# A delta-rule scan whose rounds are written in two halves, with each state product beside one piece of a score product

## The chip, the cores and the metric

The kernel runs on one core of a Trainium2 chip. Its time is the device time of one execution in microseconds; three runs of the kernel before are given, and the profile is of one execution of its own. PE is the matrix engine (PEld its weight loads), DVE the vector engine, ACT the scalar engine, POOL the general-purpose engine, SP the engine that issues most DMAs.

## The reference

One layer of a bidirectional mixer works on 128 context tokens and 2048 latent tokens of 1024 channels. A normalised and modulated input goes through one projection; half of the channels take a gated short convolution, the other half a recurrent scan with 8 heads of 64 channels, in both directions:

```python
def step(S, inp):
    r_t, w_t, k_t, v_t, kk_t, a_t = inp
    s_kk = jnp.einsum('bdhij,bdhj->bdhi', S, kk_t)
    S = (S * w_t[..., None, :] - s_kk[..., :, None] * (kk_t * a_t)[..., None, :]
         + v_t[..., :, None] * k_t[..., None, :])
    return S, jnp.einsum('bdhij,bdhj->bdhi', S, r_t)

s_final, ys = lax.scan(step, s0.astype(f32), xs)
y = ys[:, 0] + jnp.flip(ys[:, 1], axis=1)      # after ys = jnp.moveaxis(ys, 0, 2)
```

The sum of both directions is normalised per head, gated, joined with the convolution half, multiplied with an output matrix, added to the input and normalised. Outputs are both token streams and the final context states.

## The kernel before, in words

Phase 1 computes norm, projection, convolution and the operands of the scan. Phase 3, at the end, is the output product. Phase 2 between them is the scan in chunks of 64 tokens, and the change lies there.

**Stages.** A stage takes a pair of heads (of four pairs) and eight chunks in each direction. Four blocks of eight chunks for each of four pairs, and one stage for the context, make 17 stages, numbered 0 to 16. In every stage there are two groups, `gi` 0 and 1, one for each direction, and each group's eight chunks are in two halves, n = 0 and 1, of four chunks.

**The products of a stage.** F and G (`partW`, tiles psF and psG) are products of the loaded operands, one pair of PSUM tiles (one for each group) for each half n. U and W (`partU`, psU and psW) complete the inverse of a 64 by 64 triangle from 32 by 32 blocks which POOL has solved (`solve`, result zt in DRAM, read back as zc, transposed on DVE as zr); ACT writes the inverse into the one buffer zb. X (`partB`, psX) multiplies F with zb, and ACT copies its negative into the buffer fg. E (`partB`, psE) multiplies parts of fg into the chunk matrices E: for each half n four pieces, two chunks of one group in each. A DVE multiplication with a mask (L1109) and an ACT copy take a piece out of PSUM, one behind the other. S (`partS`, psS) is the recurrence: for chunk i it multiplies E of that chunk with the state and the values in the tile sv, and DVE scales the result by the decay into the next chunk's sv (L1147), for which the next S waits. After chunks 3 and 7 the output half of psS goes into a tile y: copied by ACT in the first of the two visits to a block, added by DVE (L1164) in the second. T (`finish`, psT) transposes a finished y after its normalisation (DVE L1198 to L1217). S uses E of half 0 in chunks 0 to 3 and of half 1 in chunks 4 to 7.

**A round.** Round s runs the eight S of stage s and, between them, the end of `partB` of its own stage and F, G, U, W and the start of `partB` of stage s + 1. The parts are generators, and a string of letters says which generator takes its next step: L is `partW`, u and U `partU`, b `partB` of the own stage, B that of the next stage, S one chunk of `partS`, f the first three steps of a waiting `finish` and T its rest. There are three such strings: `ROUND`, `ROUND_END` for round 15, and eight S for round 16. While the flag `O.line` holds, PE takes its products in exactly this order (`mm`, `tr` and `behind`). DVE, ACT, POOL and SP are placed by a scheduler that plans the program when it is built, and each works through its own list in order.

**Buffers.** The products F, G, U, W, X, E and T take PSUM tiles from two pools in turn (`ps_tile`: two of one pool, three of the other), so that a tile can be written when the fifth one before it has been read out. From stage 14 on the pool of two is closed, and there are three. The S products have three tiles of their own. zb, zc and zr are single. The solving of stage s + 7 is written at the end of round s; POOL takes these one after the other. Its input ab is fetched by SP (L925) when the buffer of the solution two stages before is free, and what SP issues later waits behind that.

Of the kernel before, what the change touches and what calls it, by code (L numbers as in the profile page):

```python
# [745 lines left out]
NST = 17  # L746
LA = 3


ROUND = "f b L L S u b S b S S U S T U S L S B S L B B".split()  # L750
ROUND_END = "f b L L u S b S b S U S T U S L L S B S B B S".split()

def phase2(K):
    nc, tc, A, S = K.nc, K.tc, K.A, K.S
    V, G, P, T = nc.vector, nc.gpsimd, nc.scalar, nc.tensor
# [323 lines left out]
    def partB(s, st):  # L1081
        for n in range(2):
            px = [ps_tile([128, 4, 128], f"psX{s}_{gi}_{n}") for gi in range(2)]
            for i in range(4):
                for gi, g in enumerate(st.g):
                    u = half(g, n).start + i
                    for h in range(2):
                        r = place(g.d, h)
                        mm(px[gi][H[1 - h], i, :], B.zb[r, gi, u, :], g.F[n][r, i, :])
            for gi, g in enumerate(st.g):  # L1090
                for h in range(2):
                    copy(g.fs[H[1 - h], g.io, h, half(g, n)], px[gi][H[1 - h]].rearrange("p u (b t) -> p b u t", b=2), True)
            yield
            for h2 in range(2):
                for gi, g in enumerate(st.g):
                    if h2 == 0:
                        g.E.append(tl([128, 4, 2, 128], "E", 4))
                    us = half(g, n)
                    k = (h2 if g.d == 0 else 1 - h2) * 2
                    lt, rt = (g.fs, g.gs) if g.d == 0 else (g.gs, g.fs)  # L1100
                    pe = ps_tile([128, 2, 2, 128], f"psE{s}_{gi}_{n}{h2}")
                    for i in range(2):
                        u = us.start + k + i
                        for hd in range(2):
# [4 lines left out]
                    V.tensor_tensor(to(H[1]), of(H[1]), B.mE[:, g.d].unsqueeze(1).broadcast_to((128, 4, 64)), ALU.mult)  # L1109
                    copy(to(H[0]), of(H[0]))  # L1110
                yield

    def partS(s, st, nxt):

# [139 lines left out]
    def main():  # L1254
        setup_rest()
        run = lambda gen: [None for _ in gen]
        states(0, sts[0])
        sts[1] = partL(1)
        bb = B.bb
        O.line = True  # L1260
        next(bb)
        sts[2] = partL(2, K.first)
        partI(6, K.first)
        next(bb)
        sts[LA] = partL(LA, K.first)
        partI(7, O.solved)
        tail = iter(())
        for s in range(NST):
            st = sts.pop(s)
            more = s + 1 < NST  # L1270
            nil = iter(())
            W, uu = (partW(s + 1, sts[s + 1]), partU(s + 1, sts[s + 1])) if more else (nil, nil)
            own, bb = bb, partB(s + 1, sts[s + 1]) if more else nil
            todo = [pend.pop(0) for _ in range(len(pend) if s > NST - 4 else min(1, len(pend)))]
            if s == NST - 3:
                O.pm.close()
                O.pm = None
# [10 lines left out]
            gens = dict(L=W, b=own, u=uu, U=uu, B=bb, S=partS(s, st, sts.get(s + 1)))  # L1288
            for c in (ROUND if s < NST - 2 else ROUND_END if more else "S" * 8):
                if c == "f":  # L1290
                    for f in todo:
                        for _ in range(3):
                            next(f, None)
                elif c == "T":
                    for f in todo:
                        run(f)
                else:
                    next(gens[c])
                    if c == "S":
                        next(tail, None)  # L1300
# [211 lines left out]
```

## Time and profile before

| what | us |
|---|---|
| three timed runs | 1645.6, 1651.7, 1653.2 (median 1651.73) |
| span of the profiled execution, first to last instruction | 1642.5 |
| profiled execution's own time as the page gives it | the span alone, 1642.5 |
| PE busy in the span | 1531.9 (93%) |
| DVE, ACT, POOL busy | 1104.6 (67%), 762.7 (46%), 586.8 (36%) |
| first S product starts at | 1010.3 |
| last S product starts at | 1449.0 |

The scan runs from about 1010 to 1450 us; what stands ahead of it is phase 1, what follows is mostly the output product. In the rows below, a row of the timeline has the start in us, the duration, engine, line, operation, what it writes and reads, shape, how many in one run, and in brackets the engine's idle time before it with what ended that. A matrix product of F32 stands as two records, and an instruction's end on PE is modelled, so the time from the start of one group to the start of the next is what a group costs.

### The profile page before, as it was taken

To read this page: it belongs to the slowest core of one execution; us is meant where nothing else is said; L and a number is where in the kernel's file an instruction comes from. 1 tells how busy PE (TensorE), PEld (TensorE's weight loads), DVE (VectorE), ACT (ScalarE), POOL (GpSimd) and SP (SyncE) were. 2 spreads that over 40 slices of the span, in tenths; PEclk is the share of its full clock that TensorE was granted. 3 is DMA by queue.
4 is the path that set the end of the run, shared out by engine and by line. 5 is a ranking of instruction groups with operands and counts; after the bars stand their busy time and mean duration, and the time that the engine had idled before them with its cause. 6 is when DMAs were issued, how large, how long until landed. Compare 5 with 4: busy or idle time off the path is not lost.

```text
span 1642.5 us, 42385 instructions
## 1 busy us (share of the span) xinstructions
PE 1531.9 (93%) x17160; PEld 1405.2 (86%) x17160; DVE 1104.6 (67%) x2220; ACT 762.7 (46%) x1617; POOL 586.8 (36%) x1040
## 2 busy tenths in 40 slices
PE   5899999999999999999989999989999988789998
PEld 2899988999999999999988898878888876668886
DVE  5876978784738685658788794566776764574333
ACT  4554565554425452425554023757666673432222
POOL 0011211110112021102667474888888832022221
PEclk8899999999999999999999999999999998889999
DMA  9677668664746564656867858767767663264342
GB/s 377 202 272 251 237 222 300 212 230 179 236 156 195 176 210 149 203 182 203 275 203 228 285 173 256 183 166 188 215 169 202 185 160 93 66 199 166 122 151 93
DMA packets 237988, 327.23 MB, mean 199 GB/s; under 512 B 91288, under 2 KB 191896, under 8 KB 223712
## 3 DMA queue, kind: packets, MB, share of 16 engines
q1 hardware_dynamic: 231840, 318.55, 61.3%
q0 software_dynamic: 1200, 3.93, 0.6%
q8 instruction: 135, 2.21, 0.6%
q10 hardware_dynamic: 4752, 2.04, 0.5%
q14 instruction: 61, 0.50, 0.1%
HBM read 207.92 MB, written 116.54 MB: 198 GB/s over the span
## 4 chain that ended last, share of the span: by engine, by line
PE 45%; POOL 9%; DVE 8%; ACT 4%; issue 4%; DMA 3%; SPq 0%; DVEq 0%; POOLq 0%; ACTq 0%
POOL zt L950 4%; PE psu L1381 4%; PE psu L1382 4%; PE psu L1383 4%; POOL ztmp L947 3%; PE psE L840 2%; PE psS L840 2%; ACT fg L829 1%; PE mmc L166 1%; PE mmg L168 1%; PE mmg L166 1%; PE mmg L167 1%; PE mmc L167 1%; PE mmc L168 1%; PE mmv L166 1%
## 5 line engine op out<-in xcount | busy, mean ns | idle before, releaser
L950 POOL TENSOR_TENSOR zt<-zt,ztmp 128x30 f32<-128x30 f32 (+7 forms) x390 | 153.0, 392 | 30.6
L840 PE MATMUL psE<-fg 128*64 128x128 f32 x2176 | 135.4, 277 | 15.8 <-ACT fg L831 13.6
L840 PEld LDWEIGHTS psE<-fg 128*64 128x64 f32 x2176 | 120.6, 139 | 22.4 <-ACT fg L831 15.6
L840 PE MATMUL psS<-sv,E 128*64 128x64 f32 x2176 | 98.6, 233 | 19.0 <-DVE sv L1147 18.5
L840 PEld LDWEIGHTS psS<-sv,E 128*64 128x64 f32 x2176 | 81.6, 143 | 34.8 <-DVE sv L1147 24.9
L329 POOL TENSOR_TENSOR shk<-rawl 128x384 f32<-128x384 f32 (+1 forms) x24 | 23.5, 979 | 241.1 <-ACT rawl L325 221.8
L829 ACT ACTIVATE fg<-psX 64x512 f32<-64x512 f32 x136 | 80.5, 592 | 37.3 <-PE psX L840 35.2
L1448 POOL TENSOR_TENSOR z<-z,x 128x512 f32<-128x512 f32 x32 | 41.8, 1307 | 137.9 <-DVE z L1444 114.4
L947 POOL TENSOR_TENSOR ztmp<-ab,zt 128x60 f32<-128x60 f32 (+4 forms) x165 | 85.9, 521 | 12.9
L1147 DVE TENSOR_TENSOR sv<-psS,pc 64x128 f32<-64x128 f32 x254 | 63.8, 278 | 39.5 <-PE psS L840 37.6
L329 POOL TENSOR_TENSOR shv<-rawl 128x384 f32<-128x384 f32 (+1 forms) x24 | 21.3, 888 | 165.0 <-ACT rawl L325 164.8
L831 ACT COPY fg<-psG 64x256 f32<-64x256 f32 x136 | 49.9, 367 | 52.5 <-DVE fg L1048 29.0
L1048 DVE TENSOR_TENSOR fg<-psG,consts 64x256 f32<-64x256 f32 x136 | 57.4, 422 | 25.1 <-ACT fg L831 11.2
L1041 DVE TENSOR_TENSOR F<-psF,consts 128x512 f32<-128x512 f32 x68 | 44.1, 681 | 44.5 <-PE psF L840 44.5
L446 POOL COPY pcs<-pp 128x6 f32<-128x6 f32 (+1 forms) x48 | 20.9, 435 | 139.0 <-ACT pp L435 135.1
L166 PE MATMUL mmc<-h,w 128*128 128x384 f32 (+1 forms) x192 | 64.6, 336 | 5.9 <-ACT q1r L327 4.1
L1109 DVE TENSOR_TENSOR E<-psE,consts 128x256 f32<-128x256 f32 x136 | 53.2, 418 | 21.3 <-PE psE L840 19.9
L166 PE MATMUL mmg<-h,w 128*128 128x384 f32 (+1 forms) x192 | 63.6, 331 | 3.8 <-ACT q1v L327 3.8
L831 ACT COPY E<-psE 128x256 f32<-128x256 f32 x136 | 48.5, 373 | 36.8 <-DVE E L1109 27.4
L166 PE MATMUL mmb<-h,w 128*128 128x384 f32 (+1 forms) x192 | 63.3, 329 | 1.5 <-ACT ta L439 1.5
L166 PE MATMUL mmgb<-h,w 128*128 128x384 f32 (+1 forms) x192 | 64.0, 333 | 0.4 <-ACT q1r L327 0.4
L166 PE MATMUL mmv<-h,w 128*128 128x384 f32 (+1 forms) x192 | 63.4, 330 | 0.3 <-ACT q1r L327 0.3
(325 smaller groups left out, 5169.9 us busy)
## 6 DMA issues: line engine op xcount, KB each, us to landing
w<-scr_wsp SPq DMA_DIRECT2D x68, 1024.0 KB, 5.7
scr_wsp<-w SPq DMA_DIRECT2D x34, 1024.0 KB, 4.9
scr_ops<-pair SPq DMA_DIRECT2D x80, 384.0 KB, 4.5
wr<-in_win SPq DMA_DIRECT2D x34, 512.0 KB, 6.8
o<-scr_ops SPq DMA_DIRECT2D x32, 512.0 KB, 6.0
fg<-scr_ops SPq DMA_DIRECT2D x120, 128.0 KB, 3.6
x<-in_x SPq DMA_DIRECT2D x17, 512.0 KB, 8.5
wadas<-in_wada SPq DMA_DIRECT2D x8, 1024.0 KB, 13.5
```

What stands on the lines that cost most here:

```text
L166: T.matmul(ps[:, :n], w[:, 0, k], hh[:, 0, k, :n], start=k == 0, stop=False)
L829: P.activation(dst, src, AF.Copy, scale=-1.0)
L831: P.copy(dst, src)
L840: r = T.matmul(*a, start=True, stop=True, **k)
L947: eng.tensor_tensor(tv, ab[:, j:j + 2, j + 2:32].unsqueeze(1).broadcast_to((128, kn, 2, n)), zt[:, :kn, j:j + 2].unsqueeze(3).broadcast_to ...
L950: last = eng.tensor_tensor(zt[:, :kn, j + 2:32], zt[:, :kn, j + 2:32], tv[:, :, r], ALU.subtract).ins
L1048: V.tensor_tensor(g.gs[H[1 - h], g.op, h, us], ps[gi][r, :, 64:128], B.mG[r, g.d].unsqueeze(1).broadcast_to((64, 4, 64)), ALU.mult)
L1109: V.tensor_tensor(to(H[1]), of(H[1]), B.mE[:, g.d].unsqueeze(1).broadcast_to((128, 4, 64)), ALU.mult)
L1147: r = V.tensor_tensor(dst, sp[gi][0:64, q], B.pc[0:64, d, 2 * p:2 * p + 2, c:c + 1].broadcast_to((64, 2, 64)), ALU.mult)
L1381: T.matmul(ps[:], mh[:, n], hi[:, cs], start=start and n == 0, stop=False)
L1382: T.matmul(ps[:], mh[:, n], lo[:, cs], start=False, stop=False)
L1383: T.matmul(ps[:], ml[:, n], hi[:, cs], start=False, stop=stop and n == 3)
```

## The change

The three strings are written anew, and the E step of `partB` yields after each piece (one group, two chunks) and not after both groups:

```diff
-ROUND = "f b L L S u b S b S S U S T U S L S B S L B B".split()
-ROUND_END = "f b L L u S b S b S U S T U S L L S B S B B S".split()
+ROUND = "f b L L u U S b S b U S b S b B L L T S B S B S B S B".split()
+ROUND_END = "f b L L u U S b S b U S b b S B L L T S B S B S B S B B".split()
+ROUND_LAST = "S b S b S b S b".split()
```
```diff
                     V.tensor_tensor(to(H[1]), of(H[1]), B.mE[:, g.d].unsqueeze(1).broadcast_to((128, 4, 64)), ALU.mult)
                     copy(to(H[0]), of(H[0]))
-                yield
+                    yield
```
```diff
         partI(6, K.first)
-        next(bb)
+        for _ in range(3):
+            next(bb)
...
-            if s == NST - 1:
-                run(own)
+            gens = dict(L=W, b=own, u=uu, U=uu, B=bb, S=partS(s, st, sts.get(s + 1)))
+
+            def play(tokens):
...
+            if more:
+                play(ROUND if s < NST - 2 else ROUND_END)
+            else:
+                play(ROUND_LAST)
                 O.line = False
                 O.fg.close()
                 run(tail)
                 tail = K.tail()
                 for f in todo:
                     run(f)
...
+                play("S" * 4)
```

A round now reads: X of half 1, F and G of the next stage's half 0, U; four times S with an E piece of half 1 behind it, W after the second; then X of the next stage's half 0, F and G of its half 1, T; four times S with an E piece of the next stage's half 0 behind it. In round 16 the first four S alternate with the last E pieces in PE's fixed order, and four S follow with the tail. The products, masks, copies and DMAs are as many as before, of the same shapes.

In the lists below a row has line, operation, tile written and tiles read, output shape and count. The names are psX, psF, psG, psE with group, then half n (E: n and pair of chunks), psS with group and 0 (chunks 0 to 3) or 4 (chunks 4 to 7).

PE before, from the end of the bunch of X, F and G into the chunks 0 to 3 of one round and the start of chunks 4 to 7:

```order
L840 MATMUL psG_1_0_14577<-fg_9817,o_9812 64x128 x2
L840 MATMUL psS_0_0_14602<-sv_14051,E_14397 64x64 x4
L840 MATMUL psS_1_0_14608<-sv_14053,E_14409 64x64 x4
L840 MATMUL psE_0_10_14617<-fg_9816 64x128 x8
L840 MATMUL psE_1_10_14629<-fg_9817 64x128 x8
L840 MATMUL psE_0_11_14650<-fg_9816 64x128 x8
L840 MATMUL psE_1_11_14661<-fg_9817 64x128 x8
L840 MATMUL psU_14694<-zr_14614,a_9813 32x32 x32
L840 MATMUL psS_0_4_14729<-sv_14051,E_14616 64x64 x4
L847 MATMUL psT_14741<-consts,y_13702 128x2x64 x4
L840 MATMUL psW_14750<-zc_14551,zr_14614 32x32 x32
```

The pairs of S rows that stand between the last rows but read as the two above are left out. PE now, at the same place one round on:

```order
L841 MATMUL psG_1_0_15069<-fg_9817,o_10971 64x128 x2
L841 MATMUL psU_15096<-zr_15094,a_10972 32x32 x32
L841 MATMUL psS_0_0_15131<-sv_14545,E_14861 64x64 x4
L841 MATMUL psS_1_0_15137<-sv_14548,E_14883 64x64 x4
L841 MATMUL psE_0_10_15144<-fg_9816 64x128 x8
L841 MATMUL psE_1_10_15166<-fg_9817 64x128 x8
L841 MATMUL psW_15177<-zc_15043,zr_15094 32x32 x32
L841 MATMUL psE_0_11_15224<-fg_9816 64x128 x8
L841 MATMUL psE_1_11_15249<-fg_9817 64x128 x8
L841 MATMUL psX_0_0_15260<-F_15064,zb 64x128 x2
```

U stands ahead of the first S, one E piece lies between any two S (here the repeated S rows are left out again), and the second X follows the last piece directly.

DVE now, in the second half of a round whose stage copies its y by ACT, from the masks of G on to the masks of the next bunch:

```order
L1049 TENSOR_TENSOR fg_9817<-psG_1_1_15309,consts 64x256
L1216 SCALAR_TENSOR_TENSOR yo_15339<-psT_15334,gwh,sg_15002 128x512
L1148 TENSOR_TENSOR sv_14548<-psS_1_4_15349,pc 64x128
L1218 TENSOR_TENSOR yo_15339<-yo_15339,w_15011 128x512
L1110 TENSOR_TENSOR E_15355<-psE_0_00_15356,consts 128x4x64
L1199 TENSOR_REDUCE yss_15502<-w_15500 128x8
L1110 TENSOR_TENSOR E_15377<-psE_1_00_15378,consts 128x4x64
L1202 RECIPROCAL yss_15502<-yss_15502 128x8
L1203 TENSOR_TENSOR y_13267<-y_13267,yss_15502 128x512
L1056 STREAM_TRANSPOSE zr_15590<-zc_15539 128x512
L1110 TENSOR_TENSOR E_15377<-psE_1_01_15422,consts 128x4x64
L1042 TENSOR_TENSOR F_15560<-psF_0_0_15542,consts 128x512
```

All work of `finish` and the transpose zr now stand in this half, and the mask of the last E piece (psE_1_01) comes behind them. Before, the same kinds stood so around the chunks 5 to 7 and the mask of the next F:

```order
L1147 TENSOR_TENSOR sv_14548<-psS_1_4_15229,pc 64x128
L1215 SCALAR_TENSOR_TENSOR yo_15240<-psT_15235,gwh,sg_15002 128x512
L1217 TENSOR_TENSOR yo_15240<-yo_15240,w_15011 128x512
L1147 TENSOR_TENSOR sv_14545<-psS_0_4_15223,pc 64x128
L1198 TENSOR_REDUCE yss_15502<-w_15500 128x8
L1201 RECIPROCAL yss_15502<-yss_15502 128x8
L1202 TENSOR_TENSOR y_13206<-y_13206,yss_15502 128x512
L1041 TENSOR_TENSOR F_15313<-psF_0_1_15295,consts 128x512
L1041 TENSOR_TENSOR F_15315<-psF_1_1_15296,consts 128x512
L1147 TENSOR_TENSOR sv_15039<-psS_0_4_15223,pc 64x128
```

Rows that repeat are left out here too; the two masks of F stood ahead of the scaling of the last chunk but one.

More of the change, by code (lines that the diff above doesn't have):

```diff
@@ L1279, in main @@
                 tail = K.ahead()
-            if s == NST - 1:
-                run(own)
+            gens = dict(L=W, b=own, u=uu, U=uu, B=bb, S=partS(s, st, sts.get(s + 1)))
+            def play(tokens):
+                for c in tokens:
+                    if c == "f":
+                        for f in todo:
+                            for _ in range(3):
+                                next(f, None)
+                    elif c == "T":
+                        for f in todo:
+                            run(f)
+                    else:
+                        next(gens[c])
+                        if c == "S":
+                            next(tail, None)
+            if more:
+                play(ROUND if s < NST - 2 else ROUND_END)
+            else:
+                play(ROUND_LAST)
                 O.line = False
@@ L1287, in main @@
                     run(f)
[L1288 to L1300, printed above, removed]
+                play("S" * 4)
             if s + LA + 1 < NST:
```

## The prediction

> **What bounds the kernel now.** I read the busy shares first, then three stretches of the span, then one round on PE, and DVE and ACT beside it.
>
> ```profile
> 1090.00:1332.00 242.00, 219.68 (x5814) 196.96 (x5806) 176.36 (x437) 161.81 (x341) 197.86 (x434) 0.99 0.70 186
> 1332.00:1450.00 118.00, 95.80 (x1926) 81.28 (x1924) 65.72 (x165) 57.55 (x118) 25.66 (x24) 0.90 0.39 112
> 1450.00:1642.00 192.00, 181.27 (x776) 146.31 (x776) 84.22 (x135) 48.80 (x121) 41.81 (x32) 0.97 0.41 142
> ```
>
> Columns: window, length, busy us and instructions of PE, PEld, DVE, ACT, POOL, granted clock, DMA. The change acts on the scan. Its even part, 1090 to 1332, has ten transposes:
>
> ```profile
> L1055 DVE STREAM_TRANSPOSE zr<-zc 128x512 f32<-128x512 f32 x10 | 6.9, 694 | 0.0
> ```
>
> So ten rounds take 242 us, 24.2 each. PE is busy for 22.0 of that, and DVE for 17.6 by durations. One round on PE, with the bunch ahead of it:
>
> ```profile
> 1111.36 1.10 PE L840 MATMUL psX<-F,zb 64*64 64x128 f32 x32
> 1112.29 1.05 PE L840 MATMUL psF<-fg,o 64*64 64x128 f32 x32
> 1113.17 0.39 PE L840 MATMUL psG<-fg,o 64*64 64x128 f32 x4
> 1113.75 1.09 PE L840 MATMUL psG<-fg,o 64*64 64x128 f32 x28 [0.19 <-ACT fg L829]
> 1114.77 0.69 PE L840 MATMUL psS<-sv,E 128*64 128x64 f32 x16
> 1115.29 1.92 PE L840 MATMUL psE<-fg 128*64 128x128 f32 x32
> 1117.03 0.64 PE L840 MATMUL psS<-sv,E 128*64 128x64 f32 x16
> ...
> 1120.15 0.69 PE L840 MATMUL psS<-sv,E 128*64 128x64 f32 x16 [0.27 <-DVE sv L1147]
> 1120.77 1.20 PE L840 MATMUL psU<-zr,a 32*32 32x32 f32 x64
> 1121.89 0.69 PE L840 MATMUL psS<-sv,E 128*64 128x64 f32 x16
> 1122.51 0.66 PE L847 MATMUL psT<-consts,y 128*128 128x128 f32 x4
> ...
> 1127.07 1.10 PE L840 MATMUL psX<-F,zb 64*64 64x128 f32 x32 [0.20 <-ACT zb L829]
> 1129.75 0.69 PE L840 MATMUL psS<-sv,E 128*64 128x64 f32 x16 [1.57 <-DVE sv L1147]
> 1130.37 1.10 PE L840 MATMUL psG<-fg,o 64*64 64x128 f32 x32
> 1131.40 3.71 PE L840 MATMUL psE<-fg 128*64 128x128 f32 x64
> 1135.05 1.10 PE L840 MATMUL psX<-F,zb 64*64 64x128 f32 x32
> ```
>
> From X to X it is 23.7 us. The reader is to see four losses: G of the bunch goes on only when ACT has read out X (1113.17 to 1114.77 is 1.60, where a G without a wait takes 1130.37 to 1131.40, 1.03: 0.57 lost); the S that follows an S directly (0.27); X waiting for zb (0.20); and the last S (1.57). Together 2.6, so PE's own work is 21.1. Over the ten rounds the waits of S come to
>
> ```profile
> PE psS L840 <- DVE sv L1147: 12.2, 18, 2.1
> ```
>
> 1.2 a round. What is late there is DVE, in whose list two masks of F stand ahead of that scaling. Its rows also give the prices for later:
>
> ```profile
> 1116.57 0.42 DVE L1048 TENSOR_TENSOR fg<-psG,consts 64x256 f32<-64x256 f32 x1 [0.47 <-ACT fg L831]
> ...
> 1118.09 0.76 DVE L1109 TENSOR_TENSOR E<-psE,consts 128x256 f32<-128x256 f32 x2
> ...
> 1123.99 1.11 DVE L1217 TENSOR_TENSOR yo<-yo,w 128x512 f32<-128x512 f32 x1
> ...
> 1128.23 1.28 DVE L1041 TENSOR_TENSOR F<-psF,consts 128x512 f32<-128x512 f32 x2
> 1129.42 0.47 DVE L1147 TENSOR_TENSOR sv<-psS,pc 64x128 f32<-64x128 f32 x2
> ```
>
> **What the change removes.** Shape changes on PE first. S takes 0.52 when E of its own tile shape follows (1114.77 to 1115.29) and 0.62 ahead of G (1129.75 to 1130.37): 0.1 a change. In the order before I count 13 changes of tile shape a round, in the new one 8: 0.5 us less. Then the waits of S and of X for zb, 0.27 + 0.20 + 1.57 in this round. The gain if nothing replaced them is 2.5 us a round.
>
> [...]
>
> **What it adds.** I follow one new half from the start of its X as 0. The bunch is the old one, seen above, so G ends at 3.41. ACT's part of it:
>
> ```profile
> 1136.18 2.42 ACT L829 ACTIVATE fg<-psX 64x512 f32<-64x512 f32 x4 [0.19 <-PE psX L840]
> 1138.50 1.32 ACT L1072 ACTIVATE zb<-zc,consts 128x512 f32<-128x512 f32 x2
> ```
>
> Against X at 1135.05 the copies of X run from 1.13 to 3.55, zb to 4.77, and G's copies come behind.
>
> - *The second bunch.* X, F, G need six tiles and there are five: the wait of 0.57 comes twice instead of once, +0.57.
> - *U and T directly behind G.* They are the seventh tile and wait for X's second, free at 3.55 and so usable at 3.60: +0.2 in each half, +0.4.
> - *First half, S.* U takes 1.12 (1120.77 to 1121.89), S starts at 4.72, E's piece (half of 1.74) ends at 6.09. DVE has G's second pair of masks ahead of the scaling, and these wait for ACT's first copy of G, as the row at 1116.57 did, 5.2 after its X; two masks of 0.42 end at 6.08, the scaling of the first group at 6.28. S waits till 6.33, +0.25. Behind it a turn of S and E is 1.39 on PE and two scalings and a mask, about 0.8, on DVE: no wait. X of the second half starts at 12.0.
> - *Second half, S.* DVE has, from 3.3: four G masks, yo, its addition (L1217), four E masks, eight scalings, the sum, reciprocal and product of the normalisation and zr. By starts that follow each other (an E mask 0.34, a scaling 0.19, those of 0.7 us some 0.6) that is some 7.5 us and little less than what PE has there, T, four S and four E, 6.2 to 6.9. By the list: G's first pair ends at 4.2, yo (behind T, which PE does at 3.6 to 4.2) at 5.05, then a G mask to 5.4, a scaling, the last G mask to 6.0, a scaling to 6.3, the addition to 7.0, an E mask to 7.3, two scalings to 7.7. PE could start the second group of its next S at 5.8 and the S after that at 7.5, and finds them at 6.3 and 7.6 to 7.8; the last turns fit. Some +0.6 in all, and the next X comes at 10.5.
> - *The last E piece.* Its mask comes behind zr, at 11.6 on this scale, so 1.1 after the next X has started; ACT takes the copy of that piece ahead of the copies of X, which then start at 1.57 and not at 1.13: +0.44 on everything in the next half. Where the stage adds its y on DVE, two of these stand ahead too:
>
> ```profile
> L1164 DVE TENSOR_TENSOR y<-psS,y 64x512 f32<-64x512 f32 x20 | 13.9, 693 | 1.2 <-PE psS L840 0.7
> ```
>
>   Twenty in ten rounds, four in each of five: 2 x 0.6 later, so +1.6 there with a smaller slip of 0.35 in mid round. Mean of both kinds, +1.0.
>
> Added: 0.57 + 0.4 + 0.25 + 0.6 + 1.0 = 2.8. Removed: 2.5. The rest, +0.3, is less than what I can read from rows. Bounds: if DVE and ACT hide all but the tile waits, 1.0 is added and a round gains 1.5; if L1217 takes its 1.11 each time and the end of each half is late as where y is added, 1.0 is lost. I take 0 to +0.3. The other half microsecond by which 24.2 exceeds this round is irregular and kept.
>
> **What is shifted.** SP: ab blocks the queue until POOL has read its buffer.
>
> ```profile
> 1258.62 1.72 SPq L925 DMA_DIRECT2D ab<-scr_at  x4
> ```
> ```profile
> fg<-scr_ops SPq DMA_DIRECT2D x120, 128.0 KB, 3.6
> ```
>
> POOL is busy for 197.9 of the 242 us with solutions that wait for nothing of PE, so the last ab goes out at 1258.62 whatever PE does. Behind it stand operands (fg, zc) of the stage after the next, about a round away. At an unchanged round nothing is late. Were rounds 1.5 us shorter, PE would be there 13 us earlier, and some 10 us would be left for issue and the landing, 3.6 by the median above: a gain is cut by a few us at most.
>
> Rounds 14 and 15 have three tiles, and each new second bunch waits there longer: F's second tile for X's first (2.4 instead of 0.93) and E for G, some +2.5 each, +5. Against that they lose two waits:
>
> ```profile
> 1394.88 5.01 PE L840 MATMUL psE<-fg 128*64 128x128 f32 x48 [5.69 <-ACT fg L831]
> ...
> 1417.13 1.09 PE L847 MATMUL psT<-consts,y 128*128 128x128 f32 x4 [4.39 <-DVE y L1202]
> ```
>
> ```profile
> 1390.49 0.71 DVE L1055 STREAM_TRANSPOSE zr<-zc 128x512 f32<-128x512 f32 x1 [2.26 <-issue]
> ```
>
> In the first, DVE stood at zr with G's masks behind it, 2.26 us idle; nothing but the landing of zc was left to come; now W is half a round ahead of zr. In the second T came too soon behind its normalisation; now it is half a round later. I count half of 10, so 0 net. Round 16 I cost at nothing: its last S are still back to back, and its cover, the output product after 1450, has 181 of 192 us of PE busy and starts as the scan ends.
>
> **Sum.** 13 rounds by 0 to 0.3 give 0 to 4, rounds 14 to 16 give 0; start and phase 1 are the same. The profiled span of 1642.5 becomes 1642 to 1647. The page gives that execution no other time; its span lies 9.2 under the runs' median of 1651.7. Forecast for the median: 1653.
>
> **The rivals.**
>
> *Faster: S and E pieces really cover each other.* For it: S and E alternate already from 1114.77 to 1119.25 without a wait, and the 12.2 us of S waits are gone by order. Against it: there DVE had nothing else to do. It needs DVE to end its masks before the next X. 13 rounds by 1.5, less a few us by SP, and some 3 from rounds 14 and 15: 1653 - 20 = 1633.
>
> *Slower: the end of the half decides.* One mechanism: the last E mask stands behind the normalisation, zr and y, so ACT's copies of X, and with them G, U and every S behind, are late by more than 1.6 in each round. Point: when DVE ends that mask later than 1.3 us after X's start in copying stages too; a late zc under zr suffices. Price 1.0 by 13 and 5 for the rounds with three tiles: 1653 + 18 = 1671. For it: DVE is the fuller of the two in that half. Against it: the first half leaves DVE idle for some 5 us.
>
> [...]
>
> *The change does not do what it says.* PE's list has the new order; only DVE and ACT could undo it, which is the case above.
>
> **How the numbers follow.** No change: 0.40, its own range 1645 to 1661. Faster: 0.31, 1620 to 1645. Slower: 0.29, 1661 to 1680. Half a percent (8 us) is about what a measurement tells from no change here, so these are the chances of faster, same and slower. The range goes to the middle of each rival: 1633 to 1672.
>
> **What would show it.** The waits of S in ten even rounds falling from 12.2 but not to zero, with those left in the second half; G's 0.57 twice a round; ACT's copies of X starting later than 1.13 after X; rounds 14 and 15 without the waits of 5.69 and 4.39. Wrong it is if a round comes out under 23.2 (the rows' costs of DVE were too high) or over 25 (its lists hold more than I walked).

## The result: no change that matters, and the profile after

| | before | after |
|---|---|---|
| timed runs | 20 | 20 |
| median, us | 1649.22 | 1653.46 |
| lowest to highest, us | 1641.5 to 1653.4 | 1645.8 to 1661.9 |
| ratio, 95% interval | | 1.0029, 1.0015 to 1.0043 |
| profiled execution: span, us | 1642.5 | 1656.1 |

The changed kernel is slower by 0.29%, which is surely not zero and under the half percent that counts as a change here. The two profiled executions are 13.6 us apart, and that overstates the difference: the one before lies some 5 us under its median, the one after some 4 over. Of the 13.6, 2.2 had come about before the first E piece (1002.7 before, 1004.9 after), up to which PE's order is the same. The first S comes 4.3 us later than before (1014.6 against 1010.3), and the other 2.1 are the new order's own, for the most part from two causes: X waits 1.04 us for ACT there, 0.34 before, and U now stands ahead of that S:

```profile
1010.01 0.98 PE L841 MATMUL psX<-F,zb 64*64 64x128 f32 x26 [1.04 <-ACT E L832]
1013.43 1.20 PE L841 MATMUL psU<-zr,a 32*32 32x32 f32 x64
```

A round is counted from its first S to that of the next. From the first E to round 3 it takes 87.6 us before and 85.1 after, rounds 3 to 12 take 241.7 and 252.1, and from there to the start of the last chunk's S (1448.1 and 1462.3; the 1449.0 of the table ahead lies within that product) 116.2 and 120.1: 445.5 and 457.4 in all.

First the three stretches of the span after the change, in the columns of the prediction (window, length, busy us and instructions of PE, PEld, DVE, ACT, POOL, granted clock, DMA):

```profile
1090.00:1332.00 242.00, 216.98 (x5554) 191.10 (x5552) 163.58 (x413) 154.71 (x324) 200.81 (x440) 0.95 0.65 179
1332.00:1450.00 118.00, 93.56 (x1944) 78.09 (x1946) 62.44 (x153) 58.94 (x121) 20.91 (x23) 0.91 0.37 102
1450.00:1656.00 206.00, 191.09 (x946) 154.80 (x940) 96.22 (x163) 53.91 (x130) 46.54 (x34) 0.96 0.42 146
```

In the even stretch PE is as full as before (217.0 against 219.7) and does less: 5554 records against 5814. The granted clock fell from 0.99 to 0.95. Where PE stood idle is in the groups of that stretch; a row ends with the idle time ahead of the group and what ended it. Before:

```profile
L840 PE MATMUL psE<-fg 128*64 128x128 f32 x1280 | 77.3, 274 | 4.5 <-ACT fg L831 3.5 <-issue 1.0
L840 PE MATMUL psS<-sv,E 128*64 128x64 f32 x1282 | 56.4, 229 | 12.7 <-DVE sv L1147 12.2 <-issue 0.5
L840 PE MATMUL psG<-fg,o 64*64 64x128 f32 x652 | 26.4, 275 | 1.9 <-ACT fg L829 1.9
```

After:

```profile
L841 PE MATMUL psE<-fg 128*64 128x128 f32 x1232 | 87.6, 287 | 1.3 <-issue 1.3
L841 PE MATMUL psS<-sv,E 128*64 128x64 f32 x1240 | 56.9, 236 | 3.6 <-DVE sv L1148 2.9
L841 PE MATMUL psG<-fg,o 64*64 64x128 f32 x608 | 28.8, 278 | 16.3 <-ACT fg L830 12.9 <-ACT E L832 3.2
```

The waits of S for DVE fell from 12.2 to 2.9 us, as the change meant. G took their place: 1.9 before, 16.3 after, nearly all of it for ACT (12.9 + 3.2). One round of the new order on PE, from X to X:

```profile
1109.41 1.10 PE L841 MATMUL psX<-F,zb 64*64 64x128 f32 x32
1110.33 1.05 PE L841 MATMUL psF<-fg,o 64*64 64x128 f32 x32
1112.01 0.44 PE L841 MATMUL psG<-fg,o 64*64 64x128 f32 x4 [0.63 <-ACT E L832]
1113.23 1.09 PE L841 MATMUL psG<-fg,o 64*64 64x128 f32 x28 [0.78 <-ACT fg L830]
1114.45 1.20 PE L841 MATMUL psU<-zr,a 32*32 32x32 f32 x64
...
1122.84 1.10 PE L841 MATMUL psX<-F,zb 64*64 64x128 f32 x32
...
1125.32 1.09 PE L841 MATMUL psG<-fg,o 64*64 64x128 f32 x28 [0.29 <-ACT fg L830]
1126.54 0.66 PE L848 MATMUL psT<-consts,y 128*128 128x128 f32 x4
...
1129.33 0.45 PE L841 MATMUL psS<-sv,E 128*64 128x64 f32 x8 [0.32 <-DVE sv L1148]
...
1133.34 1.10 PE L841 MATMUL psX<-F,zb 64*64 64x128 f32 x32
```

Between the bunches one S waits, 0.32; in the bunches G waits 0.63, 0.78 and 0.29. What is late there is in the lists of DVE and ACT at 1109. DVE:

```profile
1107.98 0.69 DVE L1056 STREAM_TRANSPOSE zr<-zc 128x512 f32<-128x512 f32 x1
...
1108.98 0.67 DVE L1203 TENSOR_TENSOR y<-y,yss 128x512 f32<-128x512 f32 x1
1109.68 1.42 DVE L1165 TENSOR_TENSOR y<-psS,y 64x512 f32<-64x512 f32 x2
1111.12 0.42 DVE L1110 TENSOR_TENSOR E<-psE,consts 128x256 f32<-128x256 f32 x1
```

ACT:

```profile
1111.58 0.37 ACT L832 COPY E<-psE 128x256 f32<-128x256 f32 x1 [2.13 <-DVE E L1110]
1111.98 2.41 ACT L830 ACTIVATE fg<-psX 64x512 f32<-64x512 f32 x4
```

The mask of the last E piece stands behind zr, the normalisation and the addition of y. ACT waits 2.13 us for it and begins the copies of X 2.57 after X, not 1.13.

### The profile page after: what moved, and what is told of

Its sections match the earlier page's. It is cut to its first block, busy times and chain, and to the rows that moved or that the text cites. A ratio compares the mean times of both kernels' runs of the same rounds, so it can differ in the third digit from the quotient of the medians.

```text
span 1656.1 us, 42414 instructions
## 1 busy us (share of the span) xinstructions
PE 1533.6 (93%) x17160; PEld 1401.9 (85%) x17160; DVE 1105.1 (67%) x2220; ACT 765.0 (46%) x1617; POOL 589.2 (36%) x1040
## 4 chain that ended last, share of the span: by engine, by line
PE 49%; DVE 11%; ACT 7%; DMA 3%; issue 3%; POOL 1%; SPq 0%; DVEq 0%; ACTq 0%; POOLq 0%
PE psE L841 4%; ACT fg L830 4%; PE psu L1389 4%; PE psu L1390 4%; PE psu L1391 4%; PE psS L841 3%; PE psW L841 1%; PE mmg L166 1%; PE mmg L167 1%; PE mmg L168 1%; PE mmc L166 1%; PE mmv L166 1%; PE mmv L167 1%; DVE sv L1148 1%; PE mmv L168 1%
## 5 line engine op out<-in xcount | busy, mean ns | idle before, releaser
L951 POOL TENSOR_TENSOR zt<-zt,ztmp 128x30 f32<-128x30 f32 (+7 forms) x390 | 152.8, 392 | 30.6
L841 PE MATMUL psE<-fg 128*64 128x128 f32 x2176 | 152.4, 284 | 4.3 <-ACT fg L830 2.0
L841 PEld LDWEIGHTS psE<-fg 128*64 128x64 f32 x2176 | 125.4, 144 | 6.0 <-ACT fg L830 2.4
L841 PEld LDWEIGHTS psS<-sv,E 128*64 128x64 f32 x2176 | 85.0, 146 | 28.2 <-DVE sv L1148 13.8
L948 POOL TENSOR_TENSOR ztmp<-ab,zt 128x60 f32<-128x60 f32 (+4 forms) x165 | 86.7, 525 | 12.9
L1110 DVE TENSOR_TENSOR E<-psE,consts 128x256 f32<-128x256 f32 x136 | 56.6, 416 | 49.1 <-PE psE L841 47.0
L841 PE MATMUL psG<-fg,o 64*64 64x128 f32 x1088 | 52.9, 285 | 23.5 <-ACT fg L830 17.8
L841 PEld LDWEIGHTS psG<-fg,o 64*64 64x64 f32 x1088 | 37.8, 137 | 36.4 <-ACT fg L830 25.0
```

Of the source, the lines that this page charges most:

```text
L841: r = T.matmul(*a, start=True, stop=True, **k)
L948: eng.tensor_tensor(tv, ab[:, j:j + 2, j + 2:32].unsqueeze(1).broadcast_to((128, kn, 2, n)), zt[:, :kn, j:j + 2].unsqueeze(3).broadcast_to ...
L951: last = eng.tensor_tensor(zt[:, :kn, j + 2:32], zt[:, :kn, j + 2:32], tv[:, :, r], ALU.subtract).ins
```

## The experiments

Each ratio is to the kernel before, timed on the same chip; the changed kernel's is 1.0029, and a difference between ratios of 0.001 is 1.65 us.

**One product tile more.** The rotation gets six PSUM tiles, and S keeps two of its own instead of three.

```diff
-        O.p2 = Pool(K, "p2s", "left", 3, PSUM)
-        O.pS = Pool(K, "p2S", "left", 3, PSUM)
+        O.p2 = Pool(K, "p2s", "left", 4, PSUM)
+        O.pS = Pool(K, "p2S", "left", 2, PSUM)
...
-        if O.pm is not None and (O.n % 5 < 2 or O.p2 is None):
+        if O.pm is not None and (O.n % 6 < 2 or O.p2 is None):
```

> The changed kernel with six rotating product tiles instead of five; the state products keep two tiles of their own instead of three. Theory (too few tiles cost the change its gain): the wait of G for ACT's copies of X (0.57 to 0.78 us, twice a round) and that of U and T behind G (0.4 a round) go, up to 1.5 us a round over 13 rounds, so about 1653.5 - 20 = 1634 us, ratio to the kernel before about 0.99, and G's waits in the even rounds fall from 12.9 + 3.2 us to under 4. Rival (ACT and DVE are late anyway, PE only waits elsewhere): the waits move to S and E, total 1650 to 1656 us, ratio 1.000 to 1.004, waits of S up by as much as those of G fall.

Measured: 1638.4 us, ratio 0.9944 (0.9922 to 0.9966), 14 us below the changed kernel. Its groups in the same stretch, as waits (engine, tile, line, what it waited for: us, times, longest):

```profile
PE psS L841 <- DVE sv L1148: 17.3, 24, 1.4
PE psG L841 <- ACT E L832: 4.9, 7, 2.0
```

G's wait for X's read-out is gone, so it was the sixth tile that it lacked. But S waits 17.3 instead of 2.9, of which 11.0 are eight waits of 1.37, each in the first half of a round. Theory and rival each hold in part: the tile pays, and what G no longer waits S waits for DVE.

Where it pays is not where the theory looked. Rounds 3 to 12 fell from 252.1 to 244.4 us, but with 10.2 us at half clock instead of 23.5, and half of that difference is 6.6 of the 7.7 (an estimate: in the changed kernel the E piece at 1290.04 takes 1.70 us to the next S at half clock, the one at 1279.63 takes 0.88 at full). Rounds 13 to 16 fell from 120.1 to 109.7 (half clock 13.7 instead of 24.5): from stage 14 on the same edit gives four tiles in place of three.

**The same tile in the old order.** The tile edit is put on the kernel before; with two tiles for S, T has to stand ahead of the second half's first S.

```diff
-ROUND = "f b L L S u b S b S S U S T U S L S B S L B B".split()
+ROUND = "f b L L S u b S b S S T U S U S L S B S L B B".split()
```

> The kernel before with six rotating product tiles and two of S (with two, T has to stand ahead of the second half's first S and is moved there in the rounds up to 14). Theory (the old order has one bunch a round, whose wait of 0.57 goes; its other waits, of S for DVE, 1.2 a round, stay, and two tiles of S may add a wait for the read-out of y): 0 to 0.6 us a round less, 1640 to 1648 us, ratio 0.995 to 1.000: so the sixth tile is worth more to the new order than to the old. Rival (the sixth tile helps any order): 1632 to 1638 us, ratio 0.990 to 0.994.

Measured: 1637.6 us, ratio 0.9932 (0.9907 to 0.9957), 11 us below the kernel before. The theory fell: the old order gains from a sixth tile (with T moved) nearly what the new one does, and with six tiles the two orders differ by no more than the intervals. So the shortage of tiles is not what holds the new order back against the old. In the profiled executions rounds 3 to 12 gained nothing here (243.6 us instead of 241.7; less half of the half-clock time, 236.8 and 238.2), and rounds 13 to 16 fell from 116.2 to 109.0, where E's wait of 5.69 for G's masks is gone. In both orders, then, the largest part of the gain is in the end rounds, and what the ten even rounds gain is mostly clock. No run adds the tile in the even rounds alone, and the moved T was not tried alone.

**zr and the sum of squares behind the last E mask.** In DVE's list the transposition and the reduction go behind that mask.

```diff
         behind(r, O.scaled)
+        behind(r, O.emask)
...
-        V.tensor_reduce(ss[:], heads(w[:]), mybir.AxisListType.X, ALU.add)
+        behind(V.tensor_reduce(ss[:], heads(w[:]), mybir.AxisListType.X, ALU.add), O.emask)
```

> The changed kernel, with the transposition of zr and the sum of squares of the normalisation (and what follows from it) put behind the last mask of the E product in DVE's list; nothing else. Theory (the last E mask, late behind the normalisation and zr, delays ACT's copies of X: 1.0 a round, and the second half's S waits 0.6): 0.6 to 1.0 us a round less, 8 to 13 us, about 1643 us, ratio 0.994 to 0.998; in the trace the first copy of X starts no later than 1.2 us after X. Rival (the copies of X start late for ACT's own list, or U, which needs zr, is late in turn): no gain, 1652 to 1658 us, with new waits of U for DVE in each round.

Measured: 1647.8 us, ratio 1.0005 (0.9989 to 1.0021): 4 us less, where 8 to 13 were expected. Over the even stretch ACT's first copy of X begins 1.95 us after X in the mean in the changed kernel (2.30 in the bunch ahead of U, 1.59 in the one ahead of T) and 1.14 to 1.22 before. Here it is 1.77 and 1.59, 1.68 in the mean. So those two operations hold the mask by half a microsecond, and the rest of the lateness is elsewhere: in the stages that add y, and in the mask and copy of E themselves, which follow each other behind a piece that ends as X starts. G waits as before, while an S that once waited 4.9 us for scaling raises the last row:

```profile
PE psG L841 <- ACT fg L830: 13.7, 20, 1.3
PE psS L841 <- DVE sv L1150: 8.7, 13, 4.9
```

That one is a late load of w ahead of the scaling on DVE, 4.4 us, once. Whether it is late in every execution one profile does not show; it is as much as the whole measured gain, so the price of the two operations stays open between 4 and some 8 us.

**No cover.** The S products stand back to back, the E pieces behind them.

```diff
-ROUND = "f b L L u U S b S b U S b S b B L L T S B S B S B S B".split()
+ROUND = "f b L L u U S S U S S b b b b B L L T S S S S B B B B".split()
```

> The changed kernel with the E pieces taken out from between the state products: in each half the S products stand back to back and the four E pieces behind them. The number of changes of tile shape stays about the same. Theory (the E pieces cover the scaling that each S waits for): every S behind an S waits 0.27 to 0.4 us again, five or six a round, and the E masks come later still: +2 us a round, +26 us, about 1680 us, ratio 1.016 to 1.02; S waits of the even rounds rise from 2.9 to 20 us or more. Rival (cover is worth little since the pieces only move DVE's work to another moment): within 6 us of the changed kernel, ratio 1.000 to 1.006.

Measured: 1678.7 us, ratio 1.0189 (1.0168 to 1.0210). The cover is worth what the theory said.

```profile
PE psS L841 <- DVE sv L1148: 25.8, 46, 1.3
```

S waits 25.8 instead of 2.9. But G waits only 4.0 instead of 12.9, since DVE is done with its E masks when the half ends. The waits of S and G trade against each other in this kernel; and each round holds a stretch of half clock, shown further down.

**U and T a turn later.** They leave the place behind the bunch.

```diff
-ROUND = "f b L L u U S b S b U S b S b B L L T S B S B S B S B".split()
+ROUND = "f b L L u S b U S b S b U S b B L L S B T S B S B S B".split()
```

> The changed kernel with the U product of the first half and the T product of the second half moved one turn later, behind the first state product and E piece, so that they no longer stand directly behind the bunch. Theory (U and T cost 0.2 each, waiting as the seventh tile for ACT's copy of X; against that 0.1 for each of two more shape changes): 0.2 to 0.45 us a round less, 3 to 6 us, about 1649 us, ratio 0.998 to 1.001. Rival (the first S then stands where U and T stood and waits for DVE's masks, 0.3 to 0.6 a half): 5 to 12 us slower than the changed kernel, ratio 1.006 to 1.010, S waits of the even rounds from 2.9 to over 8 us.

Measured: 1643.2 us, ratio 0.9965 (0.9950 to 0.9981), 10.5 us below the changed kernel and 6 below the kernel before. The sign is the theory's, the size is about twice what it said. In the profiled executions rounds 3 to 12 take 240.6 instead of 252.1 us; 7.1 of these at half clock instead of 23.5, so about 8 of the 11.5 us are the clock, counting half of the half-clock time as lost, and 3.4 the waits, which is the 0.2 to 0.45 a round. The idle time ahead of U and T, 2.1 and 1.3 us in these rounds of the changed kernel, is gone; that of S fell from 4.2 to 1.8, and that of G grew from 17.1 to 21.1.

**Half the change.** Once the new first half with the old second one, once the reverse.

```diff
-ROUND = "f b L L u U S b S b U S b S b B L L T S B S B S B S B".split()
+ROUND = "f b L L u U S b S b U S b S b S T S L S B S L B B B B".split()
```
```diff
-ROUND = "f b L L u U S b S b U S b S b B L L T S B S B S B S B".split()
+ROUND = "f b L L S u b b S b b S S U U B L L T S B S B S B S B".split()
```

> The first half of the change alone: in the first half of a round the new turns of S and E pieces with U and W early, in the second half the order of before (state products with T, X and the halves of the second operands strewn between them, E at the end), E in four pieces throughout. Theory (by the terms of the prediction the first half removes 0.27 and perhaps 0.2 and adds 0.25 and 0.2, the second half keeps its 1.57 of the last S and gets no second bunch): no difference to the kernel before, 1644 to 1651 us, ratio 0.998 to 1.002; the waits of the last S of 1.57 are there in each round. Rival (the second bunch is what costs the change its gain): 8 us or more faster than before, ratio under 0.996.

> The second half of the change alone: in the first half of a round the order of before (S and halves of E in turn, then S after S, then U and W together), in the second half the new bunch of X, F and G with T behind it and then S and E pieces in turn. Theory (the second bunch removes 1.57 and 0.2 a round and adds 0.57, 0.2, 0.6 and some of the 1.0 of the late last mask): within 6 us of the kernel before, ratio 0.998 to 1.004; G waits for ACT's copies of X twice a round, and S after S by 0.27. Rival (the first half's early U is what loses): faster than before by 8 us or more, ratio under 0.996.

Measured: the first half alone 1659.6 us, ratio 1.0063 (1.0040 to 1.0086); the second alone 1699.3, 1.0311 (1.0285 to 1.0337). Neither fits theory or rival, and the second tells nothing on its subject: in writing U and W directly behind each other it added a wait of W for zr (8.6 us) and of X for zb (11.0). The first has a loss of another kind:

```profile
PE psS L841 <- DVE sv L1148: 11.9, 16, 1.8
PE psE L841 <- issue: 4.7, 2, 2.9
...
PE psS L841 <- issue: 2.8, 1, 2.8
PE psW L841 <- issue: 2.1, 2, 1.1
```

The waits of the second half's last S are there, as said (11.9). But PE also stands in "issue", where it waits for nothing that the profile shows. Over the scan these come to 18.8 us against 6.1 before and 8.1 after: 12.7 more than before, where the kernel lost 10.8. They return below.

**Faster rounds, and who takes them back.** Four runs start from six tiles with U alone a turn later.

```diff
-ROUND = "f b L L u U S b S b U S b S b B L L T S B S B S B S B".split()
+ROUND = "f b L L u S b U S b S b U S b B L L T S B S B S B S B".split()
```

> Six rotating product tiles and two of S, as in the earlier run, and U of the first half one turn later, behind the first S and its E piece. In the run with six tiles one S of each first half waited 1.37 for DVE, whose masks of G stood behind ACT's copies of G, and these behind those of U. Theory (with U later, ACT takes G's copies together and the masks come about 1.2 us sooner): 0.8 to 1.3 us a round less, 1638 - 13 = 1625 us, ratio about 0.986; the waits of 1.37 gone. Rival (zb's product on ACT, 1.32, ahead of G's copies sets that time, and the tiles already give all): 1634 to 1640 us, ratio 0.993 to 0.996, the S waits still above 10 us in the even rounds.

Measured: 1638.3 us, ratio 0.9938 (0.9914 to 0.9961), no better than six tiles alone. The time is the rival's, though S waits just under its 10 us (9.8 in the even stretch), and G waits 10.4 again. Rounds 4 to 6 take 22.8, 22.8 and 22.1 us, among the shortest of all runs, but rounds 8 to 11 take 25.9, 30.6, 23.1 and 25.8. The waits over the scan, and SP's list at that place, name the cause:

```profile
DVE zr L1056 <- DMA zc<-scr_zt: 11.1, 4, 7.3
```
```profile
1222.27 0.48 SPq L988 DMA_DIRECT2D sv<-scr_vt  x1
1232.03 2.83 SPq L926 DMA_DIRECT2D ab<-scr_at  x4
...
1244.68 1.32 SPq L1028 DMA_DIRECT2D zc<-scr_zt  x2
```

From 1222.75 to 1232.03 SP stood at ab, whose buffer POOL had not read; zc, with eight loads between them, landed 7.3 us too late for zr. (The 13.9 us named in an expectation below counts one such wait more, ahead of the scan.) POOL's ab comes each 27.6 us there (1232.0, 1259.5), and PE's rounds are shorter than that. So they were before the change, where ab comes each 27.7 us (1203.1, 1230.9, 1258.6) beside rounds of 24.2, but there zr never waits for zc in the scan. That rounds of 22.1 to 22.8 use up POOL's lead sooner is the likeliest reading. Two ways took ab out of the way. In one POOL issues the loads itself, one solution ahead:

```diff
+                load_I(s + 1, abs_[s + 1], O.solved, G.dma_start)
```

> Six tiles, U one turn later, and the loads of ab for the stages from 9 on issued by POOL itself, one solution ahead, in place of SP, where each stood before the loads of zc and blocked the queue until POOL had read its buffer (9.3 us at 1223 to 1232 in the run of six tiles with U later; zc behind it landed so late that DVE's zr waited 3.2, 7.3 and 0.3 us). Theory (the rounds of that kernel are at 22.1 to 22.8 but the blocked queue gives it back in rounds 8 to 11): 9 to 13 us less, 1638 - 11 = 1627 us, ratio 0.985 to 0.989; no wait of zr for zc. Rival (what is gained there is lost in POOL, which is late for the output weights, or in half-clock stretches): 1634 to 1640 us, ratio 0.991 to 0.995.

Measured: 1651.9 us, ratio 1.0022 (1.0004 to 1.0040): 14 us slower than with SP's loads, the rival's mechanism, and far above its price. Rounds 8 to 12 gained 8 us (120.1 instead of 128.3), and round 13 took 50.8 instead of 34.0:

```profile
PE psa L1400 <- POOL mhc L1392: 22.7, 1, 22.7
```

POOL came later to its splitting of the output weights (four steps at 1340.6, 1347.8, 1355.0 and 1358.4 us, against 1317.1, 1333.3, 1340.9 and 1344.4 with SP's loads), and the first output product waited 22.7 for it instead of 4.4. Two more runs carry the same edit: the order before with it, and the new order with ACT's product zb behind G's copies besides:

```diff
-            P.activation(zf[:, :, j * 32:j * 32 + 32], st.zc[:], AF.Identity, scale=B.hm[:, j:j + 1])
+            behind(P.activation(zf[:, :, j * 32:j * 32 + 32], st.zc[:], AF.Identity, scale=B.hm[:, j:j + 1]), O.gcopy)
```

> The order before with six tiles (T ahead) and the loads of ab from stage 9 on issued by POOL, as in the run beside it. Theory (the new order is worth more than the old once tiles and the queue are free): its rounds stay near 23.2, so the queue takes less from it; 1637.6 - 5 = 1633 us, ratio 0.989 to 0.992, and 4 to 9 us above the new order with the same two edits. Rival (the old order is as good with the same resources): within 3 us of the new order.

> As the new order with six tiles, U later and ab issued by POOL, and ACT's product zb out of zc (1.32) put behind the copies of G of the first half, which it stood ahead of. Theory (the masks of G's second pair, and with them the S of the first half, come up to 1.3 us sooner; one S of each first half still waits 0.4 to 0.9): 0.3 to 0.6 us a round less, 4 to 8 us below the run without it, ratio 0.981 to 0.985. Rival (the S there wait for E masks and their own scaling): within 3 us of the run without it.

Measured: 1645.4 us, ratio 0.9979 (0.9962 to 0.9996), for the old order and 1653.7, 1.0033 (1.0014 to 1.0052), for the new. The old order pays for that edit too, with less (its first output product waits 11.2), and is some 7 us faster than the new one with it, which neither theory nor rival had. zb's place is worth nothing, as the rival said. The other way leaves ab on SP and puts it behind zc and the operands of the next round:

```diff
+            elif 3 <= s and s + 5 < NST:
+                partI(s + 5, O.half)
...
-            if 1 <= s and s + 7 < NST:
-                partI(s + 7)
```

> Six tiles and U one turn later, with the loads of ab for the stages from 8 on left on SP but put behind the loads of zc and of both halves of the operands of the next round, some 10 us later in SP's list than where they stood ahead of zc; POOL's work and its order stay. Theory (the queue that ab blocks gives back what the faster rounds gain, and in the run with ab on POOL the stall only moved to round 13 because POOL had 6 us more to do and waited 7 us more for its loads): zr no longer waits 13.9 us for zc, rounds 8 to 11 come to 23 to 24, and POOL's products of the output weights are no later than in the run with six tiles and U later: 5 to 10 us less than that run, 1638.3 - 7 = 1631 us, ratio 0.987 to 0.991. Rival (POOL's own end decides, whatever PE and SP do, and PE then waits for the output weights in round 13): 1636 to 1641 us, ratio 0.992 to 0.996, with PE waiting over 8 us for the weights there.

Measured: 1649.9 us, ratio 1.0005 (0.9985 to 1.0024). zr waits for zc no more, rounds 8 to 11 take 101.3 instead of 105.4 us, and the gain is lost all the same: PE waits 6.3 for the weights, and rounds 4 to 7 take 99.9 instead of 91.6, with PE in "issue" in nearly each:

```profile
PE psU L841 <- issue: 5.9, 4, 1.9
PE psS L841 <- issue: 4.8, 5, 1.7
PE psE L841 <- issue: 3.4, 3, 1.9
...
PE psW L841 <- issue: 2.5, 2, 2.3
```

19.1 us over the scan in all kinds, against 6.2 without the edit. Theory and rival both missed that. Of all versions the three with six tiles and SP's loads of ab where they were, in either order, are the fastest, 0.6 to 0.7% below the kernel before.

## Why the prediction came out right, point by point

*Forecast and sum.* 1653 was forecast and 1653.5 measured. That they agree to half a microsecond is luck: the base, 1651.7, was the median of three runs where twenty gave 1649.2, so the change forecast was 1.3 us (0 to 4 by the sum) and the change measured 4.2.

The sum said 0 to 0.3 us a round more, over 13 rounds (it leaves one of the 17 out). The ten rounds 3 to 12 went from 24.17 to 25.21 us; without the time lost at half clock (estimated as half of 6.8 and of 23.5 us) from 23.8 to 24.0, +0.2. The rounds among them that ran wholly at full clock take 24.0 before (eight) and 24.1 after (five). So the balance of the waits was right there, and the clock was not in the sum.

The two sides of that balance were each too large by almost 1 us a round, and that they cancelled is luck as well. In the even stretch the idle time ahead of S, E and W fell by 9.1, 3.2 and 2.3 us, 1.5 a round, where with the shape changes 2.5 was to go. Ahead of G, U and T it grew by 14.4, 1.9 and 1.3, 1.8 a round, where 2.8 was to come. On the side of the gain the 0.27 and 1.57 of S came from the one round shown, though the waits of S over ten rounds gave 1.2.

*The waits of S.* To fall from 12.2 but not to zero, with the rest in the second half: 2.9, and in the round shown the one wait is there. The added terms of 0.25 and 0.6 were too high, since 0.3 a round is all that S waits: DVE ends its masks and scalings in time for the turns, though not for the end of the half.

*G's tile wait and the late mask.* G now waits 16.1 us for ACT against 1.9, 1.5 a round more. The terms for it were 0.57 for the second bunch and 1.0 for late copies; as idle time of G their sum is right, and the chain named (mask behind zr, normalisation and y; ACT's copy of E ahead of X's) is what the rows at 1109 show. Its parts were off: at a round's end the copies begin 1.95 instead of 1.57 after X where y is copied, 2.6 where y is added (2.8 was the walk), and in the middle of a round 1.99 where y is added, where 1.48 was walked. In the mean of the ten rounds the copies begin 2.3 and 1.6 us after the two X, so they are late by 1.6 a round in all, not 1.0. The run with zr and the sum moved shows that these two hold only a part of it. That six tiles were wanted where there are five is borne out by G's waits for ACT: 16.1 us with two bunches on five tiles, 1.9 with one, 4.9 with two on six. In time it is not: the sixth tile pays 0.7 to 0.9% in both orders, the largest part of it in the end rounds.

*U and T behind G.* 0.2 a half. The idle time ahead of U and T in rounds 3 to 12 is 2.1 and 1.3 us, 0.17 a half, and nothing in the run with both later: right. That this order loses 10 us in time against that run was not foreseen; most of that is clock.

*Shape changes.* 0.5 a round was never measured alone. In the rounds wholly at full clock PE is busy for 21.7 us before and 21.6 after, so hardly more than 0.1 of it is seen.

*SP and POOL.* "If rounds were 1.5 us shorter, a gain is cut by a few us at most." The changed kernel never came there; the runs that did lost more: rounds 8 to 11 gave back some 10 us at ab, and each way round it a like amount elsewhere.

*Rounds 14 to 16.* Here the term failed. The wait of E for G's masks, 5.69, is gone. T's, to vanish as well, grew from 4.39 to 6.12:

```profile
1408.71 0.44 PE L841 MATMUL psF<-fg,o 64*64 64x128 f32 x4 [1.58 <-ACT E L832]
1410.27 1.64 PE L841 MATMUL psF<-fg,o 64*64 64x128 f32 x26 [1.12 <-ACT fg L830]
...
1435.00 1.09 PE L848 MATMUL psT<-consts,y 128*128 128x128 f32 x4 [6.12 <-DVE y L1203]
```

In the end round two stages are finished, and their normalisation stands on DVE behind the second bunch's masks (y at 1434.16). The waits for tiles came about, with F at 1.58 and 1.12 in one bunch, and dearer than priced: F and E wait 8.3 us for ACT in rounds 14 to 16 where, besides the 5.69, they waited 1.1, and 5 more was the price. Rounds 13 to 16 took 120.1 us instead of 116.2, of which 1.5 is half of 3 us more at half clock; 0 was forecast.

*The rivals.* The faster one needed DVE to end its masks before the next X; the last mask ends 0.5 to 2.2 us after X has started. The slower one asked for that mask to end later than 1.3 us after X at the end of rounds that copy y too, and for more than 1.6 us of lateness in each round. There the mask ends after 1.1 to 1.3, and the copies of X are late by 0.8, by 1.5 where y is added: the rival came close.

*The clock.* Not in the sum at all. In the 20 runs of the changed kernel the mean clock is 0.971, in the runs of the kernel before beside the experiments 0.972 to 0.974; across the changed kernel's own runs 0.01 of clock goes with 8.4 us. That makes 1 to 2.5 of the 4.2 us, the waits the rest; the two cannot be told apart better than that.

## What to carry to other kernels

A wait that an order removes can go to whatever the order then bunches: here S's waits for DVE fell from 12.2 to 2.9 us and G's for ACT rose from 1.9 to 16.1, and most runs moved the loss without removing it. The added buffer took G's wait away and gave it to S (4.9 and 17.3 us); the largest part of what it gained came in the last rounds, which have the fewest tiles. Price a new order at the end of each half, where the last piece's read-out meets the first read-out of the next bunch, and count how many tiles that moment needs. Before shortening a round, look for the engines that run ahead at a pace of their own, since here a queue that waited 9.3 us for POOL brought zc 7.3 us late and took the gain back some rounds later.

## What the hardware showed that was not expected

**Half clock followed where waits fell together.** Two pairs of windows of the changed kernel, in each pair one step of the clock records (3.41 us) and what follows it:

```profile
1181.70:1185.10 3.40, 1.91 (x60) 1.43 (x52) 2.55 (x6) 1.86 (x5) 2.97 (x6) 1.00 0.81 265
1185.10:1188.50 3.40, 2.97 (x114) 2.69 (x116) 2.92 (x6) 3.31 (x7) 2.89 (x7) 1.00 0.81 220
1284.15:1287.56 3.41, 1.71 (x42) 1.23 (x44) 2.59 (x5) 3.28 (x7) 2.94 (x7) 1.00 0.75 202
1287.56:1294.39 6.83, 6.83 (x128) 6.49 (x122) 3.33 (x10) 3.98 (x9) 5.93 (x17) 0.50 0.39 126
```

With PE busy for 1.91 of 3.40 us the clock stayed at 1.00; after the one with 1.71 of 3.41 it was at 0.50 for the next 6.8. PE's work took about twice as long there: the E piece at 1290.04 took 1.70 to the next S, the one at 1279.63 0.88. No sharp edge lies between the two, since one window went to half clock with more work in it (2.08 us) than the first above:

```profile
1256.85:1260.25 3.40, 2.08 (x74) 1.62 (x72) 1.97 (x4) 3.33 (x7) 2.88 (x7) 1.00 0.97 318
1260.25:1267.10 6.85, 6.49 (x105) 6.09 (x106) 2.77 (x8) 2.90 (x7) 6.03 (x16) 0.50 0.49 151
```

Over the scans of all fourteen profiles, windows at full clock in which PE was idle for less than 1 us were followed by half clock 8 times in 1343, from 1.5 to 1.75 us 17 times in 38, and above 2.1 us 42 times in 42 (before and after alone: 3 in 195, 3 in 6, 7 in 7). These are counts of this case, and what sets the clock back is not shown. G's waits come to 1.41 us in the bunch shown at 1109 and 1.80 in that at 1284, about the idle time of the second of these classes; rounds 10 to 12 after the change, with 19.5 us at half clock, took 27.8, 27.3 and 25.7 us, and half of those 19.5 is the excess over 23.7 a round. The run without cover shows it at its clearest:

```profile
1174.00:1177.40 3.40, 3.29 (x48) 3.11 (x44) 3.08 (x8) 1.34 (x3) 3.01 (x6) 0.50 0.89 291
1177.40:1201.30 23.90, 20.52 (x552) 18.06 (x548) 15.25 (x38) 14.29 (x31) 20.57 (x48) 1.00 0.60 169
1201.30:1204.70 3.40, 3.40 (x42) 3.40 (x44) 2.81 (x7) 0.63 (x1) 2.93 (x7) 0.50 0.73 219
```

From 1119.4 to 1392.5 half clock starts each 27.3 us, which is eight steps of 3.41, and rounds 4 to 12 take 27.3 in the mean: the round is in step with the clock records. That these set its length is not shown.

**PE stopped beside instruction fetches.** In the run with ab behind zc, eight stops in "issue" over 1.3 us stand in the scan. At each of them the packet records show a 16 KB fetch on an instruction queue, which is taken for PE's because PE has by far the most instructions (17160 products and as many weight loads of the 42414 on the page after the change). It started 0.2 to 1.2 us before the stop and ended between its begin and 0.7 us into it; such fetches come each 5.9 us, so that by chance one stop in six would have one. That PE had run out of instructions there is the likeliest reading, not a shown one. Why PE stops so in some orders and hardly in others ("issue" over the scan goes from nothing in the run with the second half alone to 19.1 us here) is open. The median landing of SP's loads is slower in this run than with U later and ab left in place (fg 5.6 us against 4.1, sv 8.2 against 4.3, from 1100 to 1250 us), but no run separated the two.
